# A hybrid decoder layer on one core: weight halves to VectorE, pinned splits, roots on ScalarE, three norm tiles on VectorE alone

## The chip, the cores and the metric

The kernel runs on one core of a Trainium2 chip, as one program. The metric is the time of one execution on the device in microseconds; lower is better. TensorE (PE) multiplies matrices into PSUM, VectorE (DVE) and ScalarE (ACT) read PSUM and SBUF, GpSimd (POOL) works on SBUF, and SyncE (SP) issues most of the DMAs. Each engine works through its own queue in order and waits there for semaphores of the others.

## The reference

One decoder layer over 1024 tokens of width 1024, in float32, with three parts, each closed by a residual sum (factor 2 ** 0.25) and a layer norm.

```python
z = h @ w_in                                   # h = layer_norm(x)
y_ssm = s5_mixer(z[..., :512], ...)            # diagonal state space, gelu, then g * sigmoid(g @ w_glu + b_glu)
y_gla = gla_mixer(...)                         # 4 heads of gated linear attention
h = layer_norm(DN_ALPHA * h + concat([y_ssm, y_gla]) @ w_out, ln1_g, ln1_b)
h = layer_norm(DN_ALPHA * h + memory_cross_attention(h, mem_n, w_mq, w_mkv, w_mo), ln2_g, ln2_b)
h = layer_norm(DN_ALPHA * h + square(relu(h @ w_ff1)) @ w_ff2, ln3_g, ln3_b)
```

Inside the linear attention each head's output `o` (128 wide) is normed by its own root mean square, `o * rsqrt(mean(o * o) + 1e-5)`, and multiplied by a gate. The cross-attention has 4 heads over 256 memory tokens.

## The kernel before

**Arithmetic.** A float32 operand is split into a high half (`act(hi, src)`, a rounding copy on ScalarE, L148) and a low half (source minus high half: `tt` at L142 on VectorE or POOL, or `stt` at L145 on VectorE where a scale is applied). A product of two such operands is three matmuls, high-high, high-low and low-high (`mm3`, L163). So each operand of TensorE passes ScalarE and then VectorE or POOL.

**Who does what.** `eng(bits, i)` gives VectorE where bit `i` of a constant is set and POOL where it is not. The constants at the top (MW1, MV1, MO1, OE, KE and so on) choose so for each low half and product.

**Order.** The code is traced in one order, and a planner then sets the order of each engine's queue, by when an operation's inputs are ready in its own model; what is ready sooner is issued sooner, even if it is traced later. `behind()` (L131 to L133) gives every operation of a block that runs on VectorE an edge to the VectorE operation traced last before the block: it is queued behind it and doesn't wait for its end. The block's operations on other engines get no edge.

**The stages around the change.** `Filler` holds streams of TensorE work that other stages draw on to fill TensorE's time.

1. `mem_stream` prepares one head of the cross-attention after another. `mem_load` (key weights, `mem_w(h * 256)`, and `w_mq`), `mem_wqT` (transposes), `mem_proj` for the keys (tile kvT), `mem_w(D + h * 256)` for the value weights, four products to `a_d`, the `w_mo` weights, `mem_proj` for the values (kvT again), four products to `vw_d`. `mem_w` loads two pieces of 128x1024 and splits each. Head 0 runs at the start with MW and MV0; heads 1, 2 and 3 run with MW1 and MV1, from about 313 us to 445 us.
2. `glu_stream` makes the state space half's gate (8 blocks) and then splits its result into the operand `ya` by eight calls of `y_split` (tile y from Y). It alternates with `mem_stream`, one step each. `out_stream` (the output projection's first half, L163 `ps_d<-hl,y`) comes behind both.
3. Meanwhile the linear attention's scores are made: two `diagonal` blocks, then seven levels in two halves each (`level`). A level takes 16 matmuls (`scores`, L1080), masked copies on VectorE (L1125), then scales Q (tile g, half on VectorE, half on POOL) and K (tile qk, mostly POOL) for the next level. Between two halves `fill.run(GB)` traces 5 us by its own count of streams 1 and 2. So of the eight `y_split` calls the first is traced just before the second half of level 0, the second and third behind it, the fourth behind the first half of level 1, and the last four behind the values' `mem_proj` split of head 1 and the key weights of head 2.
4. Then come ten steps over the eight token tiles of 128. Step `tk` runs `gla_chunk(tk)` (L1173, L1175: products; four Square activations with a sum; the root; the scaling of the four heads; the gate), `gla_out(tk - 1)` (transposes, L1197, and the split into `ya`), and two output blocks of tile `tk - 2`. The second of these ends in `layer_norm` of the first norm, and `transposes` (L258, with its split into tile h) follow three blocks later.
5. `dense(h1, a_d, softmax_epi, ...)` follows, the attention's scores with the softmax, on the same tile order; then the second projection with the second norm (`ahead=True`), and the MLP, which takes the rest.

**The root before.** `rsqrt` runs on VectorE on 128x4: one tensor-scalar for mean plus epsilon, one for a first guess from the bits, and three Newton rounds of three operations.

**The norm.** `layer_norm` has three forms. Plain: the first operation (subtract the mean, times the gain) in full width on VectorE, then the lower half's scale and bias on VectorE, the upper half's scale on ScalarE and its bias on POOL. Light: VectorE works on the lower half alone, and ScalarE (scale and shift) and POOL (gain, bias) on the upper half. Alone: both operations in full width on VectorE. GLN is 53, so bits 0, 2, 4 and 5 are set.

Of the kernel before, what the change touches and what calls it, by code (L numbers as in the profile page):

```python
# [7 lines left out]
F32 = mybir.dt.float32  # L8
# [9 lines left out]
P = 128  # L18
# [26 lines left out]
MWU = 7  # L45
MQK = 3
MVV = 11
MW1 = 0
MV1 = 1
MO1 = 3  # L50
MQ0 = 255
ON = 206
# [29 lines left out]
def hybrid_layer(  # L82
# [52 lines left out]
    def ts(e, o, i, s1, s2=None, op0=ALU.mult, op1=None):  # L135
        if s2 is None:
            e.tensor_scalar(out=o, in0=i, scalar1=s1, scalar2=None, op0=op0)
        else:
            e.tensor_scalar(out=o, in0=i, scalar1=s1, scalar2=s2, op0=op0, op1=op1)  # L139

    def tt(e, o, a, b, op):
        e.tensor_tensor(out=o, in0=a, in1=b, op=op)  # L142

    def stt(e, o, a, s, b, op0, op1):
        e.scalar_tensor_tensor(out=o, in0=a, scalar=s, in1=b, op0=op0, op1=op1)  # L145
# [4 lines left out]
    def split(hi, lo, src, scale=None, e=nc.vector):  # L150
        if scale is None:
            act(hi, src)
            tt(e, lo, src, hi.bitcast(F32), ALU.subtract)
        else:
            act(hi, src, scale=scale)
            stt(V, lo, src, scale, hi.bitcast(F32), ALU.mult, ALU.subtract)
# [3 lines left out]
    def mm3(o, lhs, rhs, first, last, more=False):  # L160

        for n, (i, j) in enumerate(P3):
            PE.matmul(o, lhs(i), rhs(j), start=first and n == 0, stop=last and n == 2, skip_group_check=more)  # L163

    def rsqrt(e, y, v, t):
        ts(e, y.bitcast(I32), v.bitcast(I32), -0.5, 1597463007.0, ALU.mult, ALU.add)
        for _ in range(3):
            stt(e, t, y, -0.5, y, ALU.mult, ALU.mult)
            tt(e, t, t, v, ALU.mult)
            stt(e, y, t, 1.5, y, ALU.add, ALU.mult)  # L170

    def rsqrt1(y, v, eps, t):

# [828 lines left out]

    def y_split(th, k):
        hi, lo = (ya(0, th)[:, i, k, :].rearrange("p (c t) -> p c t", t=T) for i in range(2))
        split(hi, lo, Y0[:, k, :].rearrange("p (t c) -> p c t", t=T)[:, th * 64:(th + 1) * 64, :], scale=0.25)

    R = []

    def res(t):
        return R[t // 4][:, t % 4, :]  # L1010
# [70 lines left out]


    prod = y1f[:, 0:2048].rearrange("p (a t) -> p a t", a=2)
    ones2 = const.tile([P, 2], F32, name="ones2")
    G.memset(ones2, 0.0)
    for h in range(2):
        G.memset(ones2[hrow[h], h:h + 1], 1.0)

# [74 lines left out]
    def gla_chunk(tk):  # L1163
        ktm, on, sr, vt = K[:, :, tk * P:(tk + 1) * P], Am[:, tk].rearrange("p h t -> p (h t)"), sr_[tk % 2], v_[tk % 2]
        if tk < NT - 1:
            up = bank("s", (P, 2, P))
            for a in range(2):
                for h in range(2):
                    PE.matmul(up[hrow[h], a, :], ktm[:, a, h * 64:h * 64 + 64],
                              vt[:, (2 * a + h) * P:(2 * a + h + 1) * P], start=True, stop=True)  # L1170
        po = bank("g", (P, 4, P))
        for h in range(4):
            PE.matmul(po[:, h, :], Am[:, tk, h, :], vt[:, h * P:(h + 1) * P], start=True, stop=tk == 0)  # L1173
            if tk:
                PE.matmul(po[:, h, :], Q[:, h // 2, h % 2, tk * P:(tk + 1) * P], S[:, h // 2, :], start=False, stop=True)  # L1175
        if tk < NT - 1:
            tt(G, S, S, dcl[:, :, tk:tk + 1].to_broadcast([P, 2, P]), ALU.mult)
            tt(V, S, S, up, ALU.add)
        if tk < NT - 2:
            gla_keys(tk + 1)  # L1180
        sq = small.tile([P, 12], F32, tag="sq", name="sq")
        for h in range(4):
            act(on[:, h * P:(h + 1) * P], po[:, h, :], AF.Square, accum_out=sq[:, h:h + 1])
        ts(V, sq[:, 0:4], sq[:, 0:4], 1.0 / P, EPS, ALU.mult, ALU.add)
        rsqrt(V, sq[:, 4:8], sq[:, 0:4], sq[:, 8:12])
        if ON >> tk & 1:
            for h in range(4):
                act(on[:, h * P:(h + 1) * P], po[:, h, :], scale=sq[:, 4 + h:5 + h])
        else:
            on4 = on.rearrange("p (h v) -> p h v", h=4)  # L1190
            tt(V, on4, po, sq[:, 4:8].unsqueeze(2).to_broadcast([P, 4, P]), ALU.mult)
        tt(eng(OE, tk), on, on, sr, ALU.mult)
# [31 lines left out]
    def post_norm(put, rows, scale=ALPHA, ahead=False):  # L1224

        half = stage.tile([P, NT, 2, 6], F32, tag="cn", bufs=1, name="half") if ahead else None

        def epi(n, t, po):
            r = res(t)[:, n * 512:(n + 1) * 512]
            if scale is None:  # L1230
                tt(V, r, r, po, ALU.add)
            else:
                stt(V, r, r, scale, po, ALU.mult, ALU.add)
            if n == 0:
                if ahead:
                    V.bn_stats(out=half[:, t, 0, :], in_=r)
                late.append(lambda: None)
            else:
                layer_norm(res(t), rows, GLN >> t & 1, half[:, t] if ahead else None, ahead and t > 4)
                late.append(lambda: put(t))  # L1240
        return epi

# [493 lines left out]
```

## Time and profile before

| | |
|---|---|
| time, median of 3 runs | 1400.96 us (1398.86 to 1404.36) |
| profiled execution, whole | 1396.52 us |
| its span, first to last instruction | 1394.7 us |
| TensorE busy (matmul) | 1336.5 us, 96% |
| VectorE busy | 976.8 us, 70% |
| ScalarE busy | 567.2 us, 41% |
| POOL busy | 447.2 us, 32% |
| granted TensorE clock, mean | 0.988 |

The views quoted below are of the profiled execution. A row of a timeline has its start (us from the span's first instruction), its duration in us, the engine, the line, the operation, the tiles written and read, the shape and the count; in brackets stands how long the engine sat idle before it and what ended that. A row of a group has busy time, mean duration in ns and the idle time ahead of it. PEld is TensorE's weight load, which runs beside the matmuls. A line such as L142 is that of a helper, so the tile's name tells what the operation is for.

### The profile page before, as it was taken

The numbers are of one execution on the slowest core, as the hardware profiler recorded it, in microseconds if no ns is written. First come the engines' busy times: TensorE is split into PE (matmuls) and PEld (weight loads), VectorE is DVE, ScalarE is ACT, GpSimd is POOL, SyncE is SP. The second block draws the span as 40 slices with busy tenths as digits, with TensorE's granted clock in tenths as the row PEclk, the third lists the DMA queues.
The fourth block names the chain that finished last, engine by engine and source line by source line (L and its number), as shares of the span: only waits on it lengthen the run. The fifth ranks groups of instructions, "written<-read, shape, count | busy, mean of one in ns | idle before, by whom it ended". The sixth has DMA issues, their size and how long they took to land. (4 is left out here: it accounts for less than half of the span.)

```text
span 1394.7 us, 18871 instructions
## 1 busy us (share of the span) xinstructions
PE 1336.5 (96%) x6824; PEld 1108.8 (80%) x6824; DVE 976.8 (70%) x1756; ACT 567.2 (41%) x943; POOL 447.2 (32%) x330
## 2 busy tenths in 40 slices
PE   6788999999899998999999999999999999999997
PEld 6575788787799887788888787888888888888886
DVE  8999588846855479844458866665655586668785
ACT  4432532343535143332213655445555343335431
POOL 1663133403855133200003223433331152003353
PEclk9899999999999999999999999999999999999999
DMA  8832332444666120310111656754446984235432
GB/s 296 266 121 68 120 106 68 140 166 136 222 224 211 53 77 23 104 34 14 61 46 32 195 173 206 234 166 158 147 142 224 327 309 166 91 106 160 142 106 91
DMA packets 155514, 199.81 MB, mean 143 GB/s; under 512 B 16295, under 2 KB 86045, under 8 KB 155293
## 3 DMA queue, kind: packets, MB, share of 16 engines
q1 hardware_dynamic: 143536, 179.44, 39.7%
q10 hardware_dynamic: 11884, 19.17, 3.7%
q8 instruction: 54, 0.88, 0.3%
q14 instruction: 40, 0.32, 0.1%
HBM read 140.38 MB, written 58.20 MB: 142 GB/s over the span
## 5 line engine op out<-in xcount | busy, mean ns | idle before, releaser
L163 PE MATMUL ps_d<-xt,w1q 128*128 128x512 f32 x576 | 137.4, 389 | 0.5 <-DVE hid L142 0.5
L163 PEld LDWEIGHTS ps_d<-xt,w1q 128*128 128x128 f32 x576 | 108.0, 188 | 23.3 <-DVE hid L142 0.9
L142 POOL TENSOR_TENSOR hl<-raw,hl 128x1024 fp32r<-128x1024 f32 x21 | 62.8, 2997 | 167.9 <-ACT hl L148 167.9
L163 PE MATMUL ps_s<-cell 128*128 128x512 f32 x432 | 113.1, 389 | 0.0
L163 PE MATMUL ps_d<-cell 128*128 128x512 f32 x432 | 106.0, 389 | 0.5 <-DVE hid L142 0.5
L163 PE MATMUL ps_d<-h0T,hl 128*128 128x512 f32 x384 | 92.3, 398 | 5.8 <-DVE hl L142 5.8
L163 PE MATMUL ps_d<-hl,y 128*128 128x512 f32 x384 | 95.4, 403 | 2.5 <-DVE y L142 2.5
L163 PEld LDWEIGHTS ps_d<-cell 128*128 128x128 f32 x432 | 81.0, 188 | 17.7 <-DVE hid L142 0.9
L163 PEld LDWEIGHTS ps_s<-cell 128*128 128x128 f32 x432 | 81.1, 188 | 16.8
L148 ACT ACTIVATE hl<-raw 128x1024 fp32r<-128x1024 f32 x62 | 65.1, 1062 | 68.9 <-PE ps_d L163 60.7
L163 PEld LDWEIGHTS ps_d<-h0T,hl 128*128 128x128 f32 x384 | 72.3, 191 | 25.5 <-DVE hl L142 6.2
L163 PE MATMUL ps_g<-xb,w1q 128*128 128x512 f32 x384 | 92.1, 391 | 0.0
L163 PE MATMUL ps_d<-hl,h0T 128*128 128x512 f32 x384 | 91.2, 394 | 0.8 <-DVE h0T L142 0.8
L142 POOL TENSOR_TENSOR R<-R,row 128x512 f32<-128x512 f32 x34 | 45.9, 1361 | 143.1 <-ACT R L148 140.0
L163 PE MATMUL ps_d<-hl,p 128*128 128x512 f32 x384 | 89.0, 391 | 0.0
L163 PEld LDWEIGHTS ps_d<-hl,y 128*128 128x128 f32 x384 | 72.6, 193 | 18.2 <-DVE y L142 2.9
L142 DVE TENSOR_TENSOR cell<-ha,cell 128x1024 fp32r<-128x1024 f32 x56 | 84.5, 1511 | 3.2 <-ACT cell L148 3.2
L148 ACT ACTIVATE hid<-hid 128x512 f32<-128x512 f32 x112 | 70.8, 632 | 38.8 <-DVE hid L142 37.1
L163 PEld LDWEIGHTS ps_d<-hl,h0T 128*128 128x128 f32 x384 | 71.0, 188 | 16.8 <-DVE h0T L142 1.2
L163 PEld LDWEIGHTS ps_d<-hl,p 128*128 128x128 f32 x384 | 71.6, 188 | 14.6
L163 PEld LDWEIGHTS ps_g<-xb,w1q 128*128 128x128 f32 x384 | 71.5, 188 | 14.6
L148 ACT ACTIVATE w1q<-raw 128x512 fp32r<-128x512 f32 x80 | 50.1, 629 | 69.0 <-PE ps_d L163 27.3
(293 smaller groups left out, 2834.7 us busy)
## 6 DMA issues: line engine op xcount, KB each, us to landing
g_d<-hid SPq DMA_DIRECT2D x112, 256.0 KB
ha<-g_d SPq DMA_DIRECT2D x56, 512.0 KB
raw<-in_w_ff_dram SPq DMA_DIRECT2D x40, 512.0 KB
b<-in_w_ff_dram SPq DMA_DIRECT2D x32, 512.0 KB
raw<-in_w_mkv_dram SPq DMA_DIRECT2D x16, 512.0 KB
raw<-in_w_in_dram SPq DMA_DIRECT2D x16, 512.0 KB
wq<-in_w_mq_dram SPq DMA_DIRECT2D x8, 512.0 KB
xs<-in_x_dram SPq DMA_DIRECT2D x8, 512.0 KB
```

The lines of the kernel that those rows point to most:

```text
L142: e.tensor_tensor(out=o, in0=a, in1=b, op=op)
L148: A.activation(out=o, in_=i, func=f, **kw)
L163: PE.matmul(o, lhs(i), rhs(j), start=first and n == 0, stop=last and n == 2, skip_group_check=more)
```

## The change

Four edits, in one diff:

- MW1 and MV1 go to 3: the low halves of heads 1 to 3's key weights (both pieces) and value weights (the second piece) run on VectorE in place of POOL.
- The body of `y_split` stands inside `behind()`.
- `gla_chunk` takes the root by a Sqrt activation (scale 1/128, bias a 128x1 tile that holds epsilon), a reciprocal on VectorE and one Newton round; the helper `rsqrt` goes.
- In `post_norm` the first norm (`ahead` is not set) takes the plain form for tiles 0 to 4, and the alone form for tiles 5, 6 and 7. The second norm is called as before.

```diff
-MW1 = 0
-MV1 = 1
+MW1 = 3
+MV1 = 3
...
-    def rsqrt(e, y, v, t):
-        ts(e, y.bitcast(I32), v.bitcast(I32), -0.5, 1597463007.0, ALU.mult, ALU.add)
-        for _ in range(3):
-            stt(e, t, y, -0.5, y, ALU.mult, ALU.mult)
-            tt(e, t, t, v, ALU.mult)
-            stt(e, y, t, 1.5, y, ALU.add, ALU.mult)
...
     def y_split(th, k):
         hi, lo = (ya(0, th)[:, i, k, :].rearrange("p (c t) -> p c t", t=T) for i in range(2))
-        split(hi, lo, Y0[:, k, :].rearrange("p (t c) -> p c t", t=T)[:, th * 64:(th + 1) * 64, :], scale=0.25)
+        with behind():
+            split(hi, lo, Y0[:, k, :].rearrange("p (t c) -> p c t", t=T)[:, th * 64:(th + 1) * 64, :], scale=0.25)
...
-    ones2 = const.tile([P, 2], F32, name="ones2")
+    ones2 = const.tile([P, 4], F32, name="ones2")
+    ones2, eps_c = ones2[:, 0:2], ones2[:, 2:3]
     G.memset(ones2, 0.0)
+    G.memset(eps_c, EPS)
...
-        ts(V, sq[:, 0:4], sq[:, 0:4], 1.0 / P, EPS, ALU.mult, ALU.add)
-        rsqrt(V, sq[:, 4:8], sq[:, 0:4], sq[:, 8:12])
+        rt_ = sq[:, 8:12]
+        act(rt_, sq[:, 0:4], AF.Sqrt, scale=1.0 / P, bias=eps_c)
+        V.reciprocal(sq[:, 4:8], rt_)
+        ts(V, sq[:, 0:4], sq[:, 0:4], -0.5 / P, -0.5 * EPS, ALU.mult, ALU.add)
+        tt(V, sq[:, 8:12], sq[:, 4:8], sq[:, 4:8], ALU.mult)
+        tt(V, sq[:, 8:12], sq[:, 8:12], sq[:, 0:4], ALU.mult)
+        stt(V, sq[:, 4:8], sq[:, 8:12], 1.5, sq[:, 4:8], ALU.add, ALU.mult)
...
-                layer_norm(res(t), rows, GLN >> t & 1, half[:, t] if ahead else None, ahead and t > 4)
+                layer_norm(res(t), rows, ahead and GLN >> t & 1, half[:, t] if ahead else None, t > 4)
```

## The prediction, made before the result

> **What bounds the kernel now.** TensorE is the bound, and where it is not busy there is something to win. The table of busy time in chosen stretches comes first; its columns are the stretch, its length, busy time (and count) of PE, PEld, DVE, ACT and POOL, the granted TensorE clock, the DMA share and GB/s.
>
> ```profile
> 300.00:330.00 30.00, 27.24 (x151) 22.38 (x148) 21.61 (x20) 12.27 (x18) 9.31 (x4) 1.00 0.55 187
> 360.00:380.00 20.00, 15.36 (x95) 13.61 (x94) 18.63 (x17) 9.15 (x11) 18.55 (x7) 0.91 0.68 237
> 380.00:500.00 120.00, 120.00 (x806) 107.39 (x804) 59.32 (x94) 46.17 (x93) 49.65 (x32) 1.00 0.49 161
> 520.00:545.00 25.00, 22.51 (x142) 18.81 (x141) 24.79 (x80) 9.20 (x29) 8.09 (x7) 1.00 0.12 34
> 545.00:560.00 15.00, 12.50 (x61) 10.16 (x60) 14.46 (x42) 5.59 (x20) 5.16 (x4) 0.89 0.00 1
> 560.00:580.00 20.00, 17.10 (x80) 14.15 (x79) 18.71 (x37) 10.10 (x13) 6.18 (x4) 0.91 0.25 80
> ```
>
> From 380 to 500 us TensorE has no gap, so nothing the change does there can be worth much. The other five stretches hold its gaps: 30.00 - 27.24 = 2.8, 4.6, 2.5, 2.5 and 2.9 us, 15.3 in all. In four of the five VectorE is at 93 to 99% (18.63 of 20, 24.79 of 25, 14.46 of 15, 18.71 of 20): the gaps are VectorE's queue. Of the list of TensorE's waits (total, times, longest) two rows stand here, for the first and the third stretch; the other four waits stand in brackets behind the timeline rows further down.
>
> ```profile
> PE ps_d L163 <- DVE wqT L142: 2.2, 1, 2.2
> ...
> PE ps_s L1169 <- DVE h L142: 2.5, 2, 1.3
> ```
>
> A gap of 2.5 us or more also leaves TensorE slow behind it: the granted clock is 0.91, 0.89 and 0.91 in the three stretches that have one, and 1.00 where the longest was 2.2. The timeline rows give its price.
>
> **Part 1, weight splits to VectorE and pinned y splits (300 to 380 us).** MW1 and MV1 move nine low halves of 128x1024 (three heads, two key and one value weight each) from POOL to VectorE. No DMA is added or moved; the raw buffer only comes free sooner. A group first (count, busy us, mean ns), then the timeline (start, duration).
>
> ```profile
> L142 DVE TENSOR_TENSOR hl<-raw,hl 128x1024 fp32r<-128x1024 f32 x41 | 56.8, 1390 | 19.4 <-ACT hl L148 19.0
> ...
> 315.48 3.42 DVE L142 TENSOR_TENSOR y1f<-qk 128x1024 f32<-128x1024 f32 x1
> 329.01 1.22 DVE L142 TENSOR_TENSOR y1f<-qk 128x1024 f32<-128x1024 f32 x1
> ...
> 362.40 2.47 DVE L145 SCALAR_TENSOR_TENSOR y<-Y,y 128x512 fp32r<-128x512 f32 x1
> 363.84 10.86 POOL L142 TENSOR_TENSOR hl<-raw,hl 128x1024 fp32r<-128x1024 f32 x2
> 364.71 2.54 DVE L1125 COPY_PREDICATED g<-mask,ps_g 128x512 f32<-128x512 uint8 x2
> 366.63 0.72 ACT L148 ACTIVATE kvT<-ps_d 128x512 fp32r<-128x512 f32 x1
> 367.61 4.88 DVE L145 SCALAR_TENSOR_TENSOR y<-Y,y 128x512 fp32r<-128x512 f32 x5
> 367.84 3.05 PE L1080 MATMUL ps_g<-g,qk 128*128 128x128 f32 x16 [3.25 <-DVE g L142]
> 372.40 0.68 DVE L142 TENSOR_TENSOR kvT<-ps_d,kvT 128x512 fp32r<-128x512 f32 x1
> 373.14 3.91 PE L163 MATMUL ps_d<-hl,kvT 128*128 128x512 f32 x16 [1.39 <-DVE kvT L142]
> 376.88 1.98 PE L1080 MATMUL ps_g<-g,qk 128*128 128x128 f32 x16
> ```
>
> VectorE gets 9 x 1.39 = 12.5 us more; POOL loses the nine, two of which took 10.86 us at 363.84. The same product took VectorE 3.42 us at 315 us, while POOL ran such a half, and 1.22 us at 329 us: one half on POOL took 2.2 us from VectorE there, more than the 1.39 it will cost on it. Around 320 us (two of the nine) I therefore take a gain of 0.5 us of the 2.8, with bounds from +2.8 (both products stand ahead of what TensorE waits for and nothing is won back) to -2.2 (the whole wait for wqT). The four halves after 380 us meet a VectorE that is half busy (59.32 of 120); I cost them at nothing. What hides them is TensorE's unbroken work; without it they cost their 1.39 us each.
>
> The chain at 360 to 373 us is worth more. In the code, the second and third of the eight splits come behind the second half of level 0, whose masked copies are the row at 364.71; yet both ran ahead of it, the third at 362.40 (2.47 us), the second before that (at least 1 us, as five took 4.88). The last five come behind the first half of level 1, and four of them behind the split of head 1's vT (tile kvT), yet all five (4.88 us) ran ahead of kvT (372.40), whose high half was there at 366.63 + 0.72 = 367.35. Behind the levels, the masked copies and g start about 2.47 + 1.0 = 3.5 us sooner, which takes the 3.25 us wait away, and TensorE goes straight from its last vT product (about 364.6) into L1080, done by 366.6. It then waits about 0.9 us for the high half (ScalarE's part of the splits isn't pinned), runs two products, and has the low half by 368.5, or 369.7 if a moved weight half of 1.39 stands ahead of it, instead of 373.14. The gain is 3.4 to 4.6, I take **4.0**; bounds 0 (the splits stay in the way, or another eight operations take their place) and 5.7 (the 4.6 us of gaps and 1.1 of slow clock: L1080's 16 matmuls took 3.05 against 1.98 at 376.88). The pinned splits wait for nothing new, they only queue later; their reader, the output projection's first half, starts at about 444 us, 70 us later.
>
> **Part 2, the heads' roots (480 to 560 us).** Per chunk the old root issues 6 scalar-tensor-tensor, 3 tensor-tensor and 2 tensor-scalar on VectorE; the new one 1, 2 and 1, with a reciprocal, and a Sqrt of 128x4 on ScalarE.
>
> ```profile
> L145 DVE SCALAR_TENSOR_TENSOR sq<-sq 128x4 f32<-128x4 f32 x48 | 11.7, 243 | 0.7
> L142 DVE TENSOR_TENSOR sq<-sq 128x4 f32<-128x4 f32 x24 | 5.6, 234 | 0.4
> L1277 DVE RECIPROCAL sm<-sm 128x2 f32<-128x2 f32 x16 | 2.6, 165 | 6.6 <-ACT prob L148 6.5
> L148 ACT ACT_TABLE_LOAD x9 | 11.5, 1283 | 2.2 <-issue 2.1
> L148 ACT ACTIVATION_READ_ACCUMULATOR g<-ps_g 128x1 f32 x32 | 6.9, 216 | 0.0
> ...
> 541.59 3.02 PE L163 MATMUL ps_d<-hl,y 128*128 128x512 f32 x12
> 556.17 4.14 PE L163 MATMUL ps_d<-hl,y 128*128 128x512 f32 x10 [2.50 <-DVE y L142]
> ```
>
> VectorE saves 5 x 0.243 + 0.234 = 1.45 us a chunk (the reciprocal set against the dropped tensor-scalar), 8.7 us over chunks 2 to 7, which run where VectorE is full. Now the added wait: the reciprocal waits for the Sqrt, and behind it on VectorE stand the residual sums and the y and h splits, for which TensorE waits. The first root operation already waited for ScalarE's four squares, so only the Sqrt itself is new; no row shows one. Nearest below is the 128x1 accumulator read of 0.22 us, above a table load plus that, 1.5 us; I take 0.3, as ScalarE holds the tables and 9.20 of 25 us busy leaves its queue short. Table loads: one more before the first chunk, one before the softmax, 2 x 1.28 = 2.6 us on ScalarE; TensorE's filler blocks and the three-block lag of the softmax cover them; uncovered they cost 2.6.
>
> In 520 to 545 us the gaps are 2.5 us in two waits for h; 1.45 us less VectorE per chunk cuts each, **1.5** (0 to 2.5). In 545 to 560 us y stood behind the root of chunk 7, mixed into the same queue; with 1.45 us less of it and one POOL product less beside it I put y about 2 us sooner, and with a gap of 0.5 the slow clock goes too: ten matmuls took 4.14 us where twelve take 3.02 (541.59), so 4.14 - 10/12 x 3.02 = 1.6 us were lost. Of 2.5 + 1.6 I take **3.0** (0 to 4.1).
>
> The Trainium skill, page "ScalarE: Activation LUTs", section "Table sets: the hidden batching unit", speaks against this edit: Sqrt lies in a set apart from Exp, and calls should be grouped by set. By its figure, some 2.7 us for a switch, the two switches would be 5.3 us of ScalarE, not 2.6; the trace shows only the load's 1.28.
>
> **Part 3, the first norm (500 to 590 us).** Tiles 0, 2 and 4 lose the light form (one POOL product less, the first VectorE operation full instead of half width); tiles 5, 6 and 7 go to VectorE alone.
>
> ```profile
> L145 DVE SCALAR_TENSOR_TENSOR R<-R,mv,row 128x1024 f32<-128x1024 f32 x9 | 13.1, 1459 | 0.0
> L145 DVE SCALAR_TENSOR_TENSOR R<-R,mv,row 128x512 f32<-128x512 f32 x7 | 6.1, 866 | 0.0
> L145 DVE SCALAR_TENSOR_TENSOR R<-R,tq,row 128x1024 f32<-128x1024 f32 x3 | 4.9, 1628 | 0.1
> L145 DVE SCALAR_TENSOR_TENSOR R<-R,tq,row 128x512 f32<-128x512 f32 x13 | 10.8, 827 | 0.1
> L142 POOL TENSOR_TENSOR R<-R,row 128x512 f32<-128x512 f32 x11 | 15.3, 1395 | 26.3 <-ACT R L148 23.5 <-DVE R L145 2.5
> ...
> 565.91 0.75 DVE L145 SCALAR_TENSOR_TENSOR R<-R,tq,row 128x512 f32<-128x512 f32 x1
> 566.92 3.48 POOL L142 TENSOR_TENSOR R<-R,row 128x512 f32<-128x512 f32 x2 [1.14 <-ACT R L148]
> 570.46 1.11 PE L258 MATMUL ps_s<-ident,R 128*128 128x128 f32 x4 [2.90 <-POOL R L142]
> 571.23 4.03 PE L163 MATMUL ps_d<-hl,y 128*128 128x512 f32 x12
> ```
>
> VectorE gets 0.59 us for each first operation made full (four tiles) and 0.80 for each second one (three tiles), 4.8 us (the four tiny operations of the light form that go are left out). Set against 8.7 saved, it keeps 3.9 us; POOL loses seven products of 1.4. At tile 5 the chain VectorE, ScalarE, POOL twice (565.91 to 570.40) becomes one VectorE operation of 1.63, done by 567.6; TensorE's second four transposes start 2.9 us sooner, and the 1.0 us that its next twelve matmuls lost (4.03 against 3.02) and 0.5 at the transposes go with the gap. Of 4.4 I take **2.7**, since the 0.8 us longer operation delays the residual sum behind it and VectorE stays close to full (bounds 0 and 4.4).
>
> **The sum.** 0.5 + 4.0 + 1.5 + 3.0 + 2.7 = 11.7 us. All gaps and slow clock together would be 2.8 + 5.7 + 2.5 + 4.1 + 4.4 = 19.5. The profiled execution took 1396.5 us (span 1394.7); the median of the runs is 1401.0, 4.4 above it, and I take the gain off the median: 1401.0 - 11.7 = **1389**. The three runs before lie 0.4% apart, so about 0.5%, 7 us, is what can be told from no change: faster means under 1394, slower over 1408.
>
> **Rivals.**
> - A, nothing won at 300 to 380 us: nine halves more on a VectorE that is 93% busy there fill the place of the pinned splits. For it: 18.63 of 20. Against: POOL's halves cost VectorE 2.2 us each where seen. 1401.0 - 7.2 = 1393.8. That the pin does nothing, because the operation it names ran early too, gives the same.
> - B, nothing won from the roots: the reciprocal, in order on a full VectorE, waits for a ScalarE that has other work first, and part 3's longer operations use up the rest. For it: 24.79 of 25. Against: ScalarE is busy 9.20 of 25. 1401.0 - 7.2 = 1393.8.
> - A and B: only tile 5's chain, 1401.0 - 2.7 = 1398.3.
> - C, slower: if the table set that holds Sqrt lacks the Square of the next chunk, every chunk loads twice, and root and squares stand in one chain. 2 x 1.28 x 7 chunks = 18 us, less 7.2 kept from parts 1 and 3: 1401.0 + 10.8 = 1412. It decides from three such chunks on (7.7 us, more than 7.2). Against: the two squares at 183.81 ran under the tables that the gate's Exp and Ln had left and needed no load; the load came behind them, for the Tanh. So Square lies in more than one set. The same section of the Trainium skill has the cheap functions in every set, but names relu, copy, identity and abs, not Square.
>
> ```profile
> 183.81 0.66 ACT L148 ACTIVATE s<-ps_s 128x256 f32<-128x256 f32 x2 [1.16 <-PE ps_s L859]
> 184.48 1.28 ACT L148 ACT_TABLE_LOAD   x1
> ```
>
> **Chances.** Forecast 0.50, A 0.17, B 0.17, both 0.09, C 0.07. Faster by over 0.5% is nine tenths of the forecast and half of A and B, whose times lie on the bound: 0.63. Within 0.5%: the rest of these and "both", 0.30. Slower: C, 0.07. The range goes from every gap gone, 1381 (1401.0 - 19.5), to "both", 1399; C and a little beyond either end, some 0.12, are left out.
>
> **What would show it.** Right: no POOL halves between 310 and 430 us; the kvT low half within 2 us of its high half, and no wait of L1080 over 1 us near 365; five sq operations per chunk on VectorE, exactly two loads more; VectorE under 93% and TensorE's gaps under 3 us in all between 520 and 580; L258 waiting for VectorE, not for POOL, at tile 5. Wrong: a new wait of TensorE for wqT or hl before 380 us; VectorE idle in front of the reciprocal for more than 0.5 us a chunk; a table load in each chunk; or new gaps past 590 us, from an order of the planner that changed there.

## The result and the profile after

The changed kernel takes 1385.05 us, median of 4 runs (1381.2 to 1385.14), against 1400.9 (1398.86 to 1404.36) for the kernel before: a ratio of 0.9887, 95% interval 0.9855 to 0.9918. The profiled execution took 1385.14 us, its span is 1383.3 instead of 1394.7. So the two spans lie 11.4 us apart, the two medians 15.9.

First the stretches of the prediction, of the changed kernel, with one more behind them (columns as there):

```profile
300.00:330.00 30.00, 29.53 (x158) 24.50 (x157) 18.47 (x21) 12.76 (x19) 3.62 (x2) 0.96 0.58 193
360.00:380.00 20.00, 17.51 (x109) 15.30 (x108) 19.52 (x19) 10.66 (x14) 9.37 (x5) 0.91 0.76 273
...
520.00:545.00 25.00, 25.00 (x157) 21.19 (x157) 23.56 (x63) 10.48 (x42) 8.29 (x7) 1.00 0.12 32
545.00:560.00 15.00, 15.00 (x79) 12.48 (x77) 14.60 (x35) 8.03 (x15) 4.96 (x3) 1.00 0.03 5
560.00:580.00 20.00, 18.62 (x91) 15.55 (x91) 19.66 (x43) 7.62 (x13) 0.00 (x0) 1.00 0.49 154
580.00:700.00 120.00, 120.00 (x566) 99.41 (x564) 52.17 (x93) 30.93 (x84) 4.80 (x2) 1.00 0.12 36
```

The gaps were 2.8, 4.6, 2.5, 2.5 and 2.9 us; they are now 0.5, 2.5, 0, 0 and 1.4. VectorE is still full (19.52 of 20, 23.56 of 25, 14.60 of 15, 19.66 of 20), and yet TensorE hardly waits for it any more: a busy share doesn't say whether the engine is late.

Such fixed stretches slide against the work, so the following ones are cut at the work itself. **Stage one** goes from the first gate product (`ps_d<-glu,hl`) to the first product with y (`ps_d<-hl,y`): the memory stream, the gate and the levels. **Stage two** goes from the first product of the chunks (`ps_s<-ident,qk`) to the first one with wa (`ps_d<-wa,h`). The same table cut there, first the kernel before, then the changed one; the lines left out are the 32.5 us between the stages and the 156.3 us behind stage two, which have no gap:

```profile
0.00:312.50 312.50, 281.57 (x1587) 224.61 (x1588) 253.47 (x660) 121.39 (x200) 108.21 (x126) 0.97 0.47 151
312.50:444.03 131.53, 124.13 (x874) 114.44 (x873) 89.65 (x90) 61.26 (x89) 75.06 (x36) 0.99 0.58 196
...
476.54:575.10 98.56, 90.67 (x523) 75.33 (x522) 82.27 (x233) 38.55 (x124) 32.49 (x25) 0.97 0.20 59
...
731.40:1394.70 663.30, 651.31 (x2953) 538.56 (x2951) 455.90 (x602) 298.34 (x424) 213.29 (x132) 1.00 0.50 167
sum 1394.70, PE 1336.49 PEld 1108.81 DVE 976.85 ACT 567.23 POOL 447.25; mean PE 222.75 PEld 184.80 DVE 162.81 ACT 94.54 POOL 74.54
```

```profile
0.00:314.60 314.60, 283.41 (x1587) 226.56 (x1588) 253.53 (x660) 121.58 (x200) 108.03 (x127) 0.97 0.47 150
314.60:443.68 129.08, 126.12 (x874) 116.21 (x873) 92.02 (x99) 61.23 (x89) 48.26 (x27) 0.97 0.59 200
...
476.16:564.72 88.56, 87.18 (x524) 73.12 (x522) 68.49 (x176) 41.21 (x132) 26.05 (x20) 1.00 0.20 60
...
721.08:1383.30 662.22, 650.97 (x2953) 538.66 (x2951) 456.56 (x602) 298.03 (x424) 213.08 (x132) 1.00 0.50 167
sum 1383.30, PE 1336.52 PEld 1110.44 DVE 966.77 ACT 569.62 POOL 410.43; mean PE 222.75 PEld 185.07 DVE 161.13 ACT 94.94 POOL 68.40
```

A stage's time is TensorE's busy time plus its gaps. TensorE's work in each row is the same, so where busy time differs, the clock differs. TensorE is busy 1336.5 us in both executions, so all of the 11.4 us are gaps that went: stage one's fall from 131.53 - 124.13 = 7.40 to 2.96 us (4.4 won), stage two's from 7.89 to 1.38 (6.5 won), the rest gives 0.5. The clock moved time about: stage two's busy time fell by 3.5 us, that of stage one rose by 2.0, and that of the stretch ahead of it, where next to nothing is edited, by 1.8.

### The profile page after: what moved, and what is told of

Same layout as the page of the kernel before. It is cut to its first block, busy times and chain, and to the rows that moved or that the text cites. A ratio compares the mean times of both kernels' runs of the same rounds, so it can differ in the third digit from the quotient of the medians.

```text
span 1383.3 us, 18805 instructions
## 1 busy us (share of the span) xinstructions
PE 1336.5 (97%) x6824; PEld 1110.4 (80%) x6824; DVE 966.8 (70%) x1713; ACT 569.6 (41%) x950; POOL 410.4 (30%) x315
## 5 line engine op out<-in xcount | busy, mean ns | idle before, releaser
L163 PE MATMUL ps_d<-hl,y 128*128 128x512 f32 x384 | 92.4, 395 | 0.0
L142 DVE TENSOR_TENSOR hl<-raw,hl 128x1024 fp32r<-128x1024 f32 x50 | 66.4, 1336 | 21.0 <-ACT hl L148 20.5
L142 POOL TENSOR_TENSOR hl<-raw,hl 128x1024 fp32r<-128x1024 f32 x12 | 33.6, 2806 | 142.0 <-ACT hl L148 142.0
```

## The experiments

All of them in one table: TensorE's gaps and the length of each stage in the profiled execution, and the median with its ratio to the runs of the kernel before that stand beside it on the same chip (over all its runs on a chip, that kernel's median was 1399.4 to 1401.94).

| kernel | stage one: gaps, length | stage two: gaps, length | median | ratio (95%) |
|---|---|---|---|---|
| before | 7.40, 131.53 | 7.89, 98.56 | 1400.9 | |
| changed | 2.96, 129.08 | 1.38, 88.56 | 1385.05 | 0.9887 (0.9855 to 0.9918) |
| halves alone | 6.76, 132.31 | 8.32, 96.28 | 1399.05 | 0.9987 (0.9962 to 1.0012) |
| pins alone | 3.56, 128.10 | 8.35, 96.27 | 1393.28 | 0.9955 (0.9934 to 0.9975) |
| roots alone | 7.21, 131.58 | 3.04, 90.64 | 1393.64 | 0.9960 (0.9935 to 0.9984) |
| norm alone | 7.60, 131.63 | 4.45, 93.14 | 1395.22 | 0.9964 (0.9937 to 0.9991) |
| halves and pins | 2.98, 129.04 | 7.92, 99.82 | 1396.2 | 0.9970 (0.9953 to 0.9987) |
| gate product to VectorE | 10.29, 134.69 | 8.21, 101.43 | 1403.06 | 1.0023 (1.0005 to 1.0042) |
| changed, POOL product added | 2.98, 127.45 | 1.38, 88.56 | 1386.92 | 0.9896 (0.9866 to 0.9926) |
| changed, ScalarE's part pinned | 3.72, 127.85 | 1.38, 88.56 | 1387.42 | 0.9895 (0.9875 to 0.9915) |
| changed, without the halves | 3.73, 128.29 | 1.38, 88.55 | 1385.17 | 0.9882 (0.9855 to 0.9910) |
| changed, half of the halves | 2.05, 126.50 | 1.37, 88.56 | 1383.13 | 0.9866 (0.9836 to 0.9895) |
| changed, again | 2.97, 127.35 | 1.38, 88.55 | 1385.21 | 0.9886 (0.9859 to 0.9912) |

Read down the gaps and each edit has its place: they repeat within about 0.5 us wherever a stage's code is the same, but for stage one of the gate product's kernel. The lengths of stage two, with its old code, run from 96.27 to 99.82 us at equal gaps (7.9 to 8.4): that is the clock.

### One part of the change at a time

The memory weights' halves alone:

```diff
-MW1 = 0
-MV1 = 1
+MW1 = 3
+MV1 = 3
```

> The kernel before with MW1 and MV1 at 3 alone. Two landmarks are compared in all runs: stretch 1, from the first gate product (ps_d<-glu,hl) to the output projection's first product (ps_d<-hl,y), 131.5 us before and 129.1 with the whole change; stretch 2, from the chunks' first transpose (ps_s<-ident,qk) to the first product ps_d<-wa,h, 98.6 us before and 88.6 with the change. Theory 'queue' (VectorE's queue makes the gaps; the pinned splits win stretch 1, the roots most of stretch 2): the eight splits still stand ahead of kvT, so stretch 1 falls by at most 1 us, to 130.5 to 131.5; stretch 2 stays. Rival 'POOL' (the nine halves on POOL hold up VectorE and the level chain, and that is what the change won): stretch 1 falls to about 129.

Stage one's gaps fell by 0.6 us, but its length is 132.31, outside the ranges of both theories, and the run is no faster that can be told. A timeline of this kernel shows why so little comes of it:

```profile
367.99 3.88 DVE L145 SCALAR_TENSOR_TENSOR y<-Y,y 128x512 fp32r<-128x512 f32 x4
...
368.30 5.85 POOL L142 TENSOR_TENSOR g<-g,g 64x512 f32<-64x512 f32 x1 [2.90 <-PE ps_g L1080]
371.79 1.21 DVE L142 TENSOR_TENSOR hl<-raw,hl 128x1024 fp32r<-128x1024 f32 x1
...
374.34 2.90 PE L1080 MATMUL ps_g<-g,qk 128*128 128x128 f32 x12 [5.22 <-DVE g L1125]
...
375.99 0.67 DVE L142 TENSOR_TENSOR kvT<-ps_d,kvT 128x512 fp32r<-128x512 f32 x1
```

Four y splits, not pinned here, and behind them one of the moved halves still stand ahead of the masked copies, and TensorE waits 5.22 us for g in one piece. So the place in VectorE's queue is still taken, with POOL's halves gone. POOL's own half of g took 5.85 us and ended at 374.15, just before the wait did, so VectorE isn't shown to be alone in holding TensorE here.

The pins alone:

```diff
-        split(hi, lo, Y0[...], scale=0.25)
+        with behind():
+            split(hi, lo, Y0[...], scale=0.25)
```

> The kernel before with y_split pinned alone. Theory 'queue': stretch 1 falls by 1.5 to 3 us, to 128.5 to 130, and L1080 has no wait of 3 us near 365 us any more. Rival 'POOL': with the halves on POOL still there, stretch 1 stays within 0.7 us of 131.5. Stretch 2 stays at 98.6 under both.

Gaps 7.40 to 3.56 us, length 3.4 us less (128.10, a little more than the theory had), L1080's wait of 3.25 us down to 0.59, the run 0.45% faster: the queue was the cause, and POOL's halves, which all still run in this kernel, were not.

The roots alone (Sqrt, reciprocal and one Newton round, with the tile for epsilon):

```diff
-        ts(V, sq[:, 0:4], sq[:, 0:4], 1.0 / P, EPS, ALU.mult, ALU.add)
-        rsqrt(V, sq[:, 4:8], sq[:, 0:4], sq[:, 8:12])
+        act(rt_, sq[:, 0:4], AF.Sqrt, scale=1.0 / P, bias=eps_c)
+        V.reciprocal(sq[:, 4:8], rt_)
...
```

> The kernel before with the new root alone. Theory 'queue': VectorE loses 1.45 us a chunk, stretch 2 falls by 4 to 6 us, to 92.5 to 94.5; tile 5's wait for POOL (2.9 us) stays. Rival 'chain' (the roots only help behind the norm's shorter chain, or the Sqrt's way through ScalarE takes the gain back): stretch 2 falls by under 2 us. The whole time falls by about 5 us under the first, by under 2 under the second. Stretch 1 stays.

Stage two took 90.64 us, 7.9 less, more than the theory's 4 to 6. Of that, 4.9 are gaps (7.89 to 3.04), and 3.1 are TensorE's busy time, so the clock. The waits for y and h went, the one for POOL's R stayed (2.9 us).

The norm alone:

```diff
-layer_norm(res(t), rows, GLN >> t & 1, half[:, t] if ahead else None, ahead and t > 4)
+layer_norm(res(t), rows, ahead and GLN >> t & 1, half[:, t] if ahead else None, t > 4)
```

> The kernel before with the norm's forms alone. VectorE gets 4.8 us more work, POOL loses seven products. Theory 'load' (VectorE's busy time decides): only tile 5's wait goes, the rest of stretch 2 gets longer; stretch 2 falls by 1 us or rises. Theory 'lock' (a VectorE operation with two inputs in SBUF waits until the POOL product that runs beside it has ended, as the 128x1 operation of 1.77 us that ended with POOL's 2.40 us product in the trace after): each POOL product taken away gives VectorE back up to its 1.3 us; stretch 2 falls by 4 us or more.

Stage two took 93.14 us, 5.4 less than in the kernel before and 3.1 less than in the shortest profile with the old code (96.27), although VectorE was given work here: the theory of the load falls. The theory of the lock, 4 us or more, is not shown by the length: of the 5.4 us only 3.4 are gaps, most of them tile 5's own wait (2.9 us before, 0.2 here). What speaks for it is VectorE's busy time, 78.07 us instead of 82.27 (1.4 us of the fall are two h splits that now come behind the stage's end). The stage in this kernel, columns as above:

```profile
477.59:570.73 93.14, 88.69 (x523) 72.81 (x522) 78.07 (x224) 37.93 (x123) 26.60 (x20) 1.00 0.19 57
```

How the lock works is told below. The whole run gained only 0.36%; in this kernel, as with the halves alone (4.0 us) and the roots alone (3.7 us), TensorE also waits in a place 400 us further on. Its waits between 800 and 1120 us:

```profile
PE ps_s L163 <- DVE w1s L142: 3.0, 5, 0.6
PE ps_s L163 <- ACT w1q L148: 1.0, 2, 0.6
```

They make 4.0 us, and neither the kernel before nor the changed one has them. The code there isn't edited, so the planner must have ordered it differently; how the edit led to that was not followed.

### Halves and pins together

The two diffs above in one kernel.

> The kernel before with the weight halves and the pinned y splits together, and neither the roots nor the norm. Stage one is the stretch from the first gate product to the first product with y: 131.53 us before, 129.08 after, 132.31 with the halves alone, 128.10 with the pins alone. Theory 'halves in the way': the halves moved to VectorE stand ahead of kvT's low half and give back a part of what the pins gain, so the stage takes 128.8 to 129.6 us, about 1 us more than with the pins alone. Rival 'halves help': the stage takes 127.0 to 127.8 us, the sum of the pins' gain and of the earlier kvT. Whole run: 1393 +- 3 us for both, so the stage decides.

Stage one took 129.04 us, inside the range of "halves in the way", yet for another reason than that theory's. The gaps are smaller than with the pins alone (2.98 against 3.56); it is TensorE's busy time that is longer, 126.06 against 124.54 us. The halves help a little, and the clock hid it. The whole run decides nothing here: stage two, not edited, was 3.5 us longer than with the pins alone.

### Is it VectorE's load or POOL beside it?

In the kernel before, some tiny VectorE operations take as long as a POOL product. Three rows of its timeline:

```profile
563.38 2.40 POOL L142 TENSOR_TENSOR wa<-raw,wa 128x1024 fp32r<-128x1024 f32 x1 [4.41 <-ACT wa L148]
563.80 2.01 DVE L145 SCALAR_TENSOR_TENSOR tq<-tq 128x1 f32<-128x1 f32 x1
565.84 0.16 DVE L145 SCALAR_TENSOR_TENSOR tq<-mv,tq 128x1 f32<-128x1 f32 x1
```

One column takes 2.01 us and ends at 565.81, the product at 565.78; the next one takes 0.16. A first test took POOL products away:

```diff
-OE = 16
+OE = 255
```

> The kernel before with the gate product of all eight chunks on VectorE (in the kernel before only chunk 4's is there): VectorE gets seven products of some 0.68 us more, 4.8 us in a stretch where it is busy 94 to 98 per cent, and GpSimd loses seven of some 1.29 us. Stage two is the stretch from the first product of the chunks to the first product with wa: 98.56 us before. Theory 'lock' (a VectorE operation with two operands in SBUF ends only when the GpSimd product beside it ends): what the seven products cost VectorE is about what it lost while they ran beside it, so the stage takes 95 to 99 us. Rival 'load' (VectorE's own work is the bound and GpSimd's is free): the stage takes 102 to 104 us and the run 1403 to 1405 us.

101.43 us, between the two theories, and so it decides nothing: the gaps hardly moved (7.89 to 8.21), and the added length is TensorE's busy time (93.22 against 90.67), the clock again. (The run is 0.2% longer; stage one, whose code is the same, has 2.9 us more gaps there.) What it does show stands in a group of stage two (count, busy us, mean ns), here of this kernel and then of the one with the norm alone:

```profile
L145 DVE SCALAR_TENSOR_TENSOR sq<-sq 128x4 f32<-128x4 f32 x48 | 11.6, 241 | 0.6
```

```profile
L145 DVE SCALAR_TENSOR_TENSOR sq<-sq 128x4 f32<-128x4 f32 x48 | 8.8, 182 | 0.6
```

In the kernel before they took 243 ns on the mean. This is one group of four: all 88 VectorE operations of the root together took 20.0 us before, 20.4 in this kernel and 18.5 with the norm alone, where its tensor-tensor operations got longer (255 ns instead of 234). So the gate's seven products, taken away, changed nothing in the root, and the norm's five fewer took a part of it away. A cleaner pair is the kernel with the roots alone and the changed one: the same 24 operations (8 scalar-tensor-tensor, 16 tensor-tensor) take 5.8 us beside the norm's ten POOL products and 3.8 beside five. It is, in part, the norm on POOL that met the root on VectorE. What the gate's products had met is the norm's first operation: without them it took 1273 ns in full width and 742 in half, before 1548 and 958.

The opposite, one idle POOL product more in each chunk of the changed kernel:

```diff
         tt(eng(OE, tk), on, on, sr, ALU.mult)
+        tt(G, sr, sr, sr, ALU.mult)
```

> The changed kernel with one more GpSimd product in every chunk (512 elements in each of 128 partitions, SBUF times SBUF, its result is not used): GpSimd is busy some 20 per cent of the stretch, so it has room for it, and no instruction of VectorE, ScalarE or TensorE is added. Stage two took 88.56 us in the changed kernel. Theory 'lock': each added product of some 1.3 us stretches the VectorE operation beside it, so the stage takes 92 to 98 us, TensorE's waits for y, h and R come back, and VectorE operations of one column show 1 to 2 us. Rival 'load': the product runs beside VectorE and the stage takes 88 to 90 us.

88.56 us, as without it and as the rival had it: the expectation from the lock failed here. One of the eight, in the timeline:

```profile
548.53 0.68 DVE L142 TENSOR_TENSOR y<-ps_s,y 128x512 fp32r<-128x512 f32 x1
548.92 1.04 POOL L142 TENSOR_TENSOR qk<-qk 128x512 f32<-128x512 f32 x1
549.43 0.69 DVE L142 TENSOR_TENSOR R<-R,ps_d 128x512 f32<-128x512 f32 x1 [0.21 <-PE ps_d L163]
```

Seven of the eight added products (tile qk) run beside VectorE operations that read PSUM or gather the norm's statistics, which keep their 0.68 us, or beside none. Beside the first of them, a tensor-scalar of 128x4 took 0.57 us where 0.15 is usual. So it seems to matter what VectorE does at that moment; the added product also reads one tile twice, where the norm's reads two. The last test measures this by itself, in a kernel that holds nothing of the layer: chains of VectorE operations, alone and beside two POOL operations.

```python
V.tensor_tensor(out=src, in0=end[0], in1=a, op=ALU.mult)
if gop:
    mid = gop(src)       # POOL, 128x1024
    last = gop(mid)
...
for _ in range(count):
    vop(o, s, k)         # VectorE or ScalarE, 128xk, each on the one before
    s = o
```

> A kernel of its own that leaves the whole layer out and measures one thing: two GpSimd operations of 128x1024 elements, one behind the other (some 2.4 us each), with a chain of six VectorE operations of 128x4 or three of 128x512 started at the same moment, and the same chains with GpSimd idle. Theory 'lock': a VectorE operation with two operands in SBUF that meets a GpSimd product lasts until that product ends, so the first of six 128x4 products takes 2 us or more instead of 0.15 and the chain 5 us instead of 1; products with an operand in PSUM and operations with one operand keep their 0.15 and 0.7 us beside the same GpSimd work, and ScalarE keeps its own. Open in the theory: whether a GpSimd operation with one operand, or with the same operand twice, locks too. Rival 'shared by halves': both engines slow by some fixed factor while they overlap, so the 128x4 operations take 0.2 to 0.4 us each; or no effect at all, and the long operations in the layer's traces waited for something else.

The rows of the chains' last five operations of 128x4 (first the chain alone; in the second line the first of the two POOL products of 2.34 us; then the chain beside such products; beside POOL operations with one operand; with one operand in PSUM; with a single operand; on ScalarE):

```profile
6.01 0.94 DVE L141 TENSOR_TENSOR vo<-vo,w 128x4 f32<-128x4 f32 x5
...
9.15 2.34 POOL L127 TENSOR_TENSOR go<-src,b 128x1024 f32<-128x1024 f32 x1 [7.49 <-DVE src L157]
9.23 5.09 DVE L141 TENSOR_TENSOR vo<-vo,w 128x4 f32<-128x4 f32 x5
...
23.16 1.70 DVE L141 TENSOR_TENSOR vo<-vo,w 128x4 f32<-128x4 f32 x5
...
44.74 0.94 DVE L144 TENSOR_TENSOR vo<-ps,vo 128x4 f32<-128x4 f32 x5
...
54.91 5.04 DVE L147 TENSOR_SCALAR vo<-vo 128x4 f32<-128x4 f32 x5
...
65.81 1.15 ACT L153 ACTIVATE vo<-vo 128x4 f32<-128x4 f32 x5
```

Two operands in SBUF: 5.09 us instead of 0.94, a little more than both POOL products together (2.34 each). An operand in PSUM: 0.94, untouched. ScalarE: untouched. So a VectorE operation of the first kind waits a POOL product out; "shared by halves" falls. A scalar-tensor-tensor is held alike (5.02 us), and a POOL product of one tile with itself holds too (4.12 us for the chain beside two of 1.9). VectorE holds POOL as well: beside products of 128x512 on VectorE the same POOL products took 2.84 and 2.67 us. Not foreseen: a tensor-scalar with one operand in SBUF is held too (5.04 instead of 0.99), and a POOL operation with one operand holds VectorE far less (1.70).

### Stage one's waits once more

ScalarE's part of the y splits pinned as well (`behind_act()` gives the same edge to the ScalarE operation traced last):

```diff
-        with behind():
+        with behind(), behind_act():
```

> The changed kernel with the other half of the y splits, ScalarE's scaled copy, pinned as VectorE's is. In the changed kernel kvT's high half was 0.88 us late behind such copies on ScalarE, its low half another 1.57 us, and the 16 products after them took 5.54 us instead of 3.91 at a granted clock of 0.83. Theory 'clock behind the gaps': without the first gap the two merge into one of at most 1.6 us, the products run at 4 us, and stage one takes 126.5 to 128 us (129.08 in the changed kernel). Rival: the low half sets the end alone, TensorE still slows behind one gap, and stage one stays at 128.5 to 129.5 us. Whole run 1383 to 1385 us by the first, 1385 by the second.

127.85 us, in the range of the first theory; the whole run, 1387.42 us, is not (1383 to 1385). A timeline of this kernel (lines are shifted by 3):

```profile
372.18 3.93 PE L166 MATMUL ps_d<-hl,kvT 128*128 128x512 f32 x16 [1.17 <-DVE kvT L145]
...
382.25 0.98 PE L166 MATMUL ps_d<-mnT,hl 128*128 128x256 f32 x6 [2.07 <-ACT vst L151]
```

The wait for the high half is gone and the sixteen products run at full clock, but the copies now stand ahead of vst, for which TensorE waits 2.07 us. The gaps are 0.8 us more in all, and as the "changed, again" kernel shows, 127.85 is no gain. The pin moved a wait.

The halves undone in the changed kernel, and half of them undone:

```diff
-MW1 = 3
-MV1 = 3
+MW1 = 0
+MV1 = 1
```

> The changed kernel with the memory weights' halves back on GpSimd (MW1 0, MV1 1): the pins, the roots and the norm stay. Theory 'halves give nothing': stage one (first gate product to first product with y) takes 127 to 129.5 us as in the changed kernel (129.08, and 127.45 where only an idle GpSimd product was added later), TensorE waits for wqT some 2 us where it waited for kvT 2.4 us, and the run is within 2 us of the changed kernel on the same chip. Rival 'halves help with the pins': stage one is 2 to 4 us longer and the run 1387 to 1389 us. Second rival 'halves in the way': stage one is 125.5 to 127 us and the run 1381 to 1383 us.

```diff
-MV1 = 3
+MV1 = 1
```

> The changed kernel with the first set of halves on VectorE (MW1 3) and the second as it was before (MV1 1). In the changed kernel a half of the second set takes 2.15 us on VectorE right ahead of kvT's low half, for which TensorE waits 1.57 us; with the first set on GpSimd it waits 2.2 us for wqT. If both waits come from where the halves run, this one has neither: stage one takes 126 to 127.5 us and the run 1381 to 1384 us on a chip where the changed kernel takes 1385. If the planner's order of the rest moves instead, or the wait for the high half (ScalarE's copies) sets the end, it stays at 128 to 129.5 us and the run at 1385.

And the changed kernel unedited, on the same chip:

> The changed kernel once more, unedited, on the chip and beside the runs of the two before it, as their yardstick and as a measure of how far two profiles of one program differ. Both theories: 1385 +- 2 us, stage two 88.56 us (TensorE has no gap there but one); stage one 129.08 us if its slow clock behind the waits comes back in each execution, 127 to 128 us if the clock is granted by chance.

Without the halves the gaps are 0.8 us larger (3.73 against 2.97) and the median is the same, 1385.17 against 1385.21: in time, "halves give nothing" holds. With half of them, as was expected, the gaps are the smallest, 2.05 us, and so is stage one, 126.50; the median is 1383.13, 2.1 us below the changed kernel's. The two ratios' intervals overlap (0.9836 to 0.9895, 0.9859 to 0.9912), so it beats the kernel before, and is only likely to beat the changed one.

The repeated kernel shows something else. The same program, the same 24 products behind the same gap of 0.45 us, first in the changed kernel's profile, then in that of the repeat:

```profile
324.78 1.72 PE L1093 MATMUL ps_g<-ones,y1f 128*128 128x2 f32 x14 [0.45 <-DVE y1f L142]
326.36 4.31 PE L163 MATMUL ps_d<-mnT,hl 128*128 128x256 f32 x24
```

```profile
326.09 1.72 PE L1093 MATMUL ps_g<-ones,y1f 128*128 128x2 f32 x14 [0.45 <-DVE y1f L142]
327.67 3.12 PE L163 MATMUL ps_d<-mnT,hl 128*128 128x256 f32 x24
```

4.31 us in one execution, 3.12 in the other. Of the seven profiles with this order of work (gaps of 0.45 to 0.48 us), the 24 products are slow in three (4.31 to 4.61 us) and not in four (3.12 to 3.13). So the gap's length doesn't decide whether TensorE is slow behind it, and no run shows what does. Another place comes out alike each time: behind the two gaps ahead of kvT's products, sixteen of these took 5.34 to 5.54 us in all four profiles that have both gaps.

## Why the prediction was right, and where it was not

**The mechanisms held.** The time (1385.05) lies in the range and below the forecast of 1389. Of the signs: no weight half of 128x1024 on POOL is left in stage one but one of 2.4 us at its end, TensorE no longer waits for g near 365, VectorE issues five operations a chunk for the root, exactly two table loads came (11 instead of 9, 1.28 us each), there is no new gap up to 700 us, and L251 (L258 before) waits for VectorE at tile 5, 1.4 us. Groups of the changed kernel's stage two, and the loads of the whole span:

```profile
L142 DVE TENSOR_TENSOR sq<-sq 128x4 f32<-128x4 f32 x16 | 2.5, 159 | 0.1
...
L1182 DVE RECIPROCAL sq<-sq 128x4 f32<-128x4 f32 x8 | 1.4, 172 | 0.3 <-ACT sq L148 0.3
L145 DVE SCALAR_TENSOR_TENSOR sq<-sq 128x4 f32<-128x4 f32 x8 | 1.3, 159 | 0.1
```

```profile
L148 ACT ACT_TABLE_LOAD x11 | 14.1, 1283 | 2.3 <-issue 2.1
```

VectorE waits 0.3 us for eight roots together, so rival B falls, and rival C with the loads: Squares ran under the Sqrt's tables in every chunk. Rival A falls with the halves and pins together (gaps 7.40 to 2.98), and its second form, a pin that does nothing, with the pins alone.

**Halves, 0.5 us:** the number came out in gaps, 0.6 us alone (7.40 to 6.76) and 0.6 with the pins (3.56 to 2.98), but that is luck. TensorE's wait for wqT, 2.2 us, went whole, and another grew elsewhere: with the pins, those for kvT from 0.2 to 2.5 us; alone, the one for g in level 1. In time the halves brought nothing that can be told.

**Pins, 4.0 us:** right in gaps, 3.8 (7.40 to 3.56); but the step "1.00 where the longest was 2.2", which let a smaller gap leave the clock alone, failed, and so did its other half, as stage two shows below. The rows of the changed kernel:

```profile
365.90 2.06 PE L1074 MATMUL ps_g<-g,qk 128*128 128x128 f32 x16
...
367.95 0.83 ACT L148 ACTIVATE kvT<-ps_d 128x512 fp32r<-128x512 f32 x1
368.10 1.30 POOL L142 TENSOR_TENSOR g<-g,g 64x512 f32<-64x512 f32 x1 [2.90 <-PE ps_g L1074]
368.33 2.15 DVE L142 TENSOR_TENSOR hl<-raw,hl 128x1024 fp32r<-128x1024 f32 x1 [0.48 <-ACT hl L148]
368.83 0.73 PE L163 MATMUL ps_d<-hl,kvT 128*128 128x512 f32 x2 [0.88 <-ACT kvT L148]
...
370.41 0.68 DVE L142 TENSOR_TENSOR kvT<-ps_d,kvT 128x512 fp32r<-128x512 f32 x1
...
371.14 5.54 PE L163 MATMUL ps_d<-hl,kvT 128*128 128x512 f32 x16 [1.57 <-DVE kvT L142]
```

L1074 starts without a wait, and TensorE waits 0.88 us for the high half, where 0.9 was forecast. The low half came at 371.09; as this execution's stage one starts 2.1 us later (314.6 instead of 312.5), that is 369.0 by the time of before, where 368.5 to 369.7 was forecast, the latter with a moved half ahead of it. One stood there; it took 2.15 us instead of 1.39, beside POOL's g until 369.40. Counted from the stage's start, TensorE took up the sixteen products 4.1 us sooner (56.5 instead of 60.6 us). But behind the gaps of 0.88 and 1.57 us they took 5.54 us instead of 3.91, so 1.6 of these were lost again. In all, stage one is 2.45 us shorter in this profile and 4.2 in that of the repeat, where 4.5 was forecast.

The Trainium skill, page "TensorE: Matmul & The Clock Gate", section "Part 1: The HAM clock gate", has a free-running window of about 3.4 us after which an idle TensorE runs at half clock. That the same gap has both outcomes here, 4.31 and 3.12 us, fits a window that runs free. That a gap of 0.45 us is enough at all doesn't follow from the page's rule, and no run shows where the windows stood.

**Stage two, 1.5 + 3.0 + 2.7 = 7.2 us:** too small for this pair of profiles, in which 10.0 was measured: 6.5 of gaps, so all but the 1.38 at tile 5, and 3.5 of clock. Two steps failed.

The first is the price of the clock, "A gap of 2.5 us or more also leaves TensorE slow behind it", from which the sum took 1.6 us behind the wait for y. With the halves alone and with the pins alone stage two has its old code, and in their profiles the same ten matmuls behind the same gap took 2.57 and 2.56 us, where the kernel before took 4.14. The row with the pins alone:

```profile
556.85 2.56 PE L163 MATMUL ps_d<-hl,y 128*128 128x512 f32 x10 [2.50 <-DVE y L142]
```

So the term was read off one execution and is no price of the gap. Against those two profiles, at 96.3 us, the change gains 7.7 in this stage, near the 7.2, and 7.0 of it are gaps (TensorE waits there 1.6 us more for y, and 1.7 instead of 2.90 us at tile 5).

The second is the price of VectorE's work, "it keeps 3.9 us". By the prediction's own figures VectorE should have been 8 x 1.45 - 4 x 0.59 - 0.80 = 8.4 us less busy in this stage (all eight chunks, four first operations and one second made full). It is 13.8 us less busy (82.27 to 68.49), of which 1.4 are two h splits that now come behind the stage's end. The forecast used mean durations, and these hold time in which VectorE stood still beside POOL. The root's 72 operations (scalar-tensor-tensor and tensor-tensor) took 17.3 us in the kernel before (0.24 each); the 24 left take 3.8 (0.159). At 0.159 the 72 would have taken 11.4, so by this estimate 5.9 us were waiting. The norm took five of POOL's ten products there away, as these groups of stage two show, first before, then changed, and the roots took away most of what could wait for them. The prediction set the norm's 4.8 us against the roots' gain; the norm alone, with more work on VectorE, cut the gaps by 3.4 us and the roots alone by 4.9. Together they cut 6.5, less than the sum, so they take away some of the same waits.

```profile
L142 POOL TENSOR_TENSOR R<-R,row 128x512 f32<-128x512 f32 x10 | 13.8, 1377 | 17.1 <-ACT R L148 14.3 <-DVE R L145 2.5
```

```profile
L142 POOL TENSOR_TENSOR R<-R,row 128x512 f32<-128x512 f32 x5 | 6.5, 1303 | 13.6 <-ACT R L148 11.1 <-DVE R L145 2.5
```

What is left at tile 5 has a POOL product ahead of it too: there a 128x1 operation of VectorE took 1.77 us and ended, at 558.37, with POOL's product for wa, at 558.35. Whether this makes the wait of 1.38 us was not tested.

That VectorE and POOL hold each other up is stated on the Trainium skill's page "SBUF — State Buffer", section "SBUF: two separate sides": one pair of ports is shared as an exclusive lock, for the whole instruction, and a VectorE operation with two SBUF inputs is among those that need it. The runs agree beside a POOL product, 5.09 against 0.94 us. They don't beside a POOL operation with one operand: two of these took 2.77 us each, and the chain 1.70. The page names a two-port mode of VectorE as another; the tensor-scalar of 512 elements took 0.43 us alone where the product took 0.69, so that may be why it was held too, which no run here separates.

**From the span to the median:** "I take the gain off the median" gave 1389. The gain of the spans was forecast at 11.7 and is 11.4, which is luck: stage one gave 2.45 us instead of 4.5, stage two 10.0 instead of 7.2, and the rest, forecast at nothing, cost 1.0. The medians differ by 15.9 here and by 16.7 on another chip (1401.94 against 1385.21). The profiled execution of the kernel before was 4.4 us faster than its median, that of the changed kernel stands at its own. Stage two with the old code varied by 3.6 us between profiles (96.27 to 99.82), with the new code by 0.01, in six of them; but at 98.56 the one profile of the kernel before leaves only 1.3 of the 4.4 to that. Its stretch ahead of stage one, 312.5 us, took 311.1 to 319.0 in the twelve other profiles of the layer, and only one was shorter; so this may be a part. Where the slower executions of the kernel before lose their time was not seen.

**The busy share as a sign** ("VectorE under 93%" between 520 and 580) was wrong: it stayed at 94 to 98%. The kvT halves lie 2.3 us apart, not 2. And the chances of the cases add up to 0.62 for faster and 0.31 for within 0.5%, where 0.63 and 0.30 are written.

## What to carry to other kernels

Before an operation is priced by its mean, compare it with its shortest of the same shape: where a 128x4 operation has a mean of 0.24 us and one of 0.16 when POOL has less to do, a part is another engine's, and taking that engine's work away can be worth more than the work itself costs where it goes. Don't price a slow clock from one execution: the same matmuls behind the same gap can run at full speed in the next. Cut a profile where the work begins and ends, and count gaps and busy time apart: gaps answer to the edit, busy time on a clock that differs from one execution to the next doesn't, and a single profile can hide or show 2 us of it. Look at the gaps of every stage, as waits can also move to code that was not edited.

## What the runs showed of the hardware that was not expected

- VectorE beside POOL: five 128x4 operations took 5.09 us instead of 0.94 with both operands in SBUF, 5.04 instead of 0.99 with a single one (tensor-scalar), 0.94 with one in PSUM; beside a POOL operation that reads one operand 1.70, beside a product of one tile with itself 4.12. In the layer a 128x1 operation took 2.01 us.
- TensorE's clock after a gap: for the same products of the same program 4.31 us or 3.12 behind 0.45 us, and for the same ten matmuls 4.14 us or 2.56 behind 2.50 us.
- Three of the four single edits brought some 4 us of new waits (4.0, 3.7, 4.0) in the up-projection, hundreds of us behind the edited code, and all of them together none.
